# Sums of weight quarters put on VectorE one operand ahead of use, and the high parts of computed down operands put later in ScalarE's queue

## The chip, the cores and the metric

One core of a Trainium2 chip runs the whole program. The metric is the device time of one execution in microseconds (us); lower is better.

## What is computed

A two-layer encoder runs over 768 tokens (a prompt of 256 and a sample of 512, which share all weights) with width 1024. In each layer a gated convolution branch and an attention branch are mixed and added to the stream, and a feed-forward part (FFN) of width 2816 follows. The change bears on the FFN only:

```
for l in range(DEPTH):
    ...
    x = x + (ga * a + gc * c) @ w_out[l]
    h2 = rms_norm(x, g_ffn[l])
    gate, up = jnp.split(h2 @ w_gu[l], 2, axis=-1)
    x = x + (jax.nn.silu(gate) * up) @ w_down[l]
return rms_norm(x, g_final)
```

All of it is in float32.

## The kernel before

**Split products.** A float32 matrix product is made of three matmuls on parts that TensorE takes in one pass: each operand is split into a high part (ScalarE copies it into the reduced type, `act` at L211) and a low part (the operand minus its high part, `sub_lo` at L214, on GpSimd for weights and on VectorE for most activations). VectorE's calls go through the wrapper class `Vector`, so all of them have line L133.

**Seven products.** In the FFN, a product of 2x2 blocks is computed with seven block products in place of eight (m = 1 to 7). Four of the seven weight operands (m = 4, 5, 6, 7) are sums or differences of quarters of two staged weight tiles. `Quad.total` (L273) makes such a sum on VectorE, 128x512, in a tile T of pool tag H (6 slots), once per quad. `Quarter.make` (L259) asks for its operand (L260), so that a missing sum goes into VectorE's queue at that point, and then puts the high part on ScalarE (L263) and the low part on GpSimd (L264).

**Order of work.** The program is one stream of blocks, and the Python code keeps a planner's clock (`Clock`): each matmul adds its planned length, and after each step of a block (six matmuls of 384 columns, planned 0.96 us, or twelve) `tick` runs the jobs that are due and then `Weights.pump` (L337), which loads weight tiles and prepares at most one weight quarter per tick (`split`, L325) if there is room: eight quarters may be ready ahead of use. All engines run their queues in order, so what the planner puts first runs first.

**The FFN's blocks.** `gu_body` (L1025) computes one 128-wide chunk of gate and up per block: the tiles are named f0 to f21 by chunk (the first two chunks share a block, f0), with twelve matmuls for each of the seven products, in the order m = 1, 7, 6, 4, 5, 2, 3. Products 6, 5 and 3 are added into the PSUM bank of product 1, and product 4 into that of product 7. So the matmuls of m=6 wait until ScalarE has copied product 1 out (`L_silu`), those of m=4 until it has copied product 7 out (`L_fu`, L1053), those of m=5 until it has copied the bank after m=6 (L1055), and those of m=3 until VectorE has added the bank after m=5 into `L_fu` (L1060).

**Down products.** After every four chunks the down product of these four is computed in four bursts (a to d) between the following chunks: burst a (m = 1, 7) stands before f4, f8, f12, f16 and f20, burst b (6, 4) behind that chunk, then c (5, 2) and d (3). `down7` (L1115) prepares their moving operands. `prepare(m)` (L1136) makes, for m = 7, 6, 5 and 3, two differences or sums on VectorE (tiles `L_dS`, `L_silu`), and `high` (L1142) puts two high parts `L_dh` on ScalarE, from which two low parts `L_dl` on VectorE follow. For these four products `high` is due D_HIGH planner microseconds after `prepare`; for m = 1, 2, 4, whose operands exist already, it is due at once:

```
jobs[m].append(clock.later(0.0 if m in (1, 2, 4) else D_HIGH, high))
```

The results of down products are added into the residual tiles `L_x` by VectorE, four or eight additions of 128x384 per product.

**Start of the FFN.** The operands of the seven products (tiles `L_h`, from `L_hs` and `L_hr`) are made on VectorE, ScalarE and GpSimd by `ffn_norm` (L920) while the block f0 is being computed.

Names of tiles in the profile: `wq_L_wgu_0m` and `wq_L_wd4b_0m` are the high and low parts of quarters of the gate/up weights and of the weights of burst b of the chunks 4 to 7; `T_L_wgu` and `T_L_wd4b` are the sums; `st_...` are the staged weight tiles.

Of the kernel before, what the change touches and what calls it, by code (L numbers as in the profile page):

```python
# [44 lines left out]
CONV_N = ZP - 2 * PAD  # L45
# [8 lines left out]
class Clock:  # L54
# [21 lines left out]
    def tick(self):  # L76
        while self.heap and self.heap[0][0] <= self.now:
            heapq.heappop(self.heap)[2]()
        while self.dve < self.now + TAP_AHEAD and self.tap():
            pass  # L80
# [38 lines left out]
class Vector:  # L119
# [5 lines left out]
    def __getattr__(self, name):  # L125
        f = getattr(self.engine, name)

        def call(out, *args, **kw):
            n = 1
            for d in (args[0].shape if name == "tensor_reduce" else out.shape)[1:]:  # L130
                n *= d
            self.clock.vector(n / 960.0 + 0.13)
            return f(out, *args, **kw)  # L133
        return call

# [20 lines left out]
def trunk(tc, x_in, x_tok, w_a, w_qkv, w_pw, w_out, w_gu, w_down, vecs, gqk, rope, y_out):  # L156
# [4 lines left out]
    with ExitStack() as ctx:  # L161
# [51 lines left out]
        def sub_lo(engine, lo, x, hi):  # L213
            engine.tensor_tensor(lo, x, hi.bitcast(F32), op=ALU.subtract)  # L214
# [73 lines left out]
        class Weights:  # L288
# [36 lines left out]
            def split(self, engines=(nc.gpsimd,)):  # L325
                w = self.all[self.ready]
                while not self.here(w):
                    assert self.load()
                assert self.live + w.size + max(self.staged, N_WS) <= N_W
                self.live += w.size  # L330
                w.live = True
                w.make(engines)
                self.staged -= sum(stage.last is w for stage in w.stages)
                self.ready += 1
                self.next = max(self.next, clock.now + W_STEP[w.size - 1])

            def pump(self):  # L337
                while self.load():
                    pass
                if self.ready < len(self.all) and clock.now >= self.next:  # L340
                    w = self.all[self.ready]
                    if self.here(w) and self.live + w.size + max(self.staged, N_WS) <= N_W:
                        self.split()
# [285 lines left out]
        def layer_blocks(l):  # L629
# [485 lines left out]
            def down7(c0):  # L1115
# [20 lines left out]
                def prepare(m):  # L1136
# [5 lines left out]
                    def high():  # L1142
                        ops[m] = U(nm(f"dh{c0}_{m}"), F32R), U(nm(f"dl{c0}_{m}"), F32R)
                        for e, x in enumerate(src[m]):
                            hi, lo = (half(t, e) for t in ops[m])
                            act(hi, x)
                            jobs[m].append(clock.later(D_LOW + 0.5 * e, lambda x=x, hi=hi, lo=lo: sub_lo(vector, lo, x, hi)))
                    jobs[m].append(clock.later(0.0 if m in (1, 2, 4) else D_HIGH, high))

# [464 lines left out]
D_AT = 0.5  # L1614
D_EACH = 2.5
D_TAIL = 2.0
D_HIGH = 0.7
D_LOW = 0.8
A_SPLIT = (15.0, 1.5)

# [17 lines left out]
RSTD_AFTER = 5.4  # L1638
TABLES_AT = 16.0
TAP_AHEAD = 1.0  # L1640
W_STEP = (0.9, 2.9)
A_EXP = 2.2
A_REC = (4.5, 2.5)
# [91 lines left out]
```

## Time and profile before

| | |
|---|---|
| median of 3 runs | 2401.75 us (2399.19 to 2402.68) |
| the profiled execution's own time | 2401.79 us |
| its span, first to last instruction | 2400.0 us |
| TensorE busy | 2235.7 us, 93% |
| VectorE busy | 1933.2 us, 81% |
| GpSimd busy | 1285.0 us, 54% |
| ScalarE busy | 1134.3 us, 47% |
| mean granted TensorE clock | 0.972 of full speed |

The FFN of the first layer takes about 670 to 1190 us of the span, that of the second about 1858 to 2380 us. Busy time is that of instructions on the engine; "idle before" is time in which the engine had nothing running, with the instruction that ended it.

### The profile page before, as it was taken

Reading aid. Unit: us, or ns where it says so; the run is one execution under the profiler, and the core shown is the slowest. Engines: PE = TensorE matmul, PEld = TensorE weight load, DVE = VectorE, ACT = ScalarE, POOL = GpSimd, SP = SyncE. Lnnn points to the kernel's source line nnn. Section 1 sums busy time; section 2 is a strip of 40 time slices with the busy share of each in tenths; the row PEclk is TensorE's granted clock in tenths of the full one; section 3 lists DMA queues with packets and bytes.
Section 4 is the critical chain, followed back from the end, with each engine's and each line's share of the span. In section 5 each row is a group of like instructions: output and inputs, shape, how many; then the busy total and the mean of one; then the engine's idle time right before and its main releaser. Section 6 shows DMA issues by size and latency. Waiting matters only on the chain. (4 is left out here: it accounts for less than half of the span.)

```text
span 2400.0 us, 34938 instructions
## 1 busy us (share of the span) xinstructions
PE 2235.7 (93%) x13276; PEld 2101.9 (88%) x13276; DVE 1933.2 (81%) x2480; ACT 1134.3 (47%) x2281; POOL 1285.0 (54%) x956
## 2 busy tenths in 40 slices
PE   8888898999979999999998899999999799999997
PEld 7878787888979999999987788878889799999997
DVE  5899999855387798798978999997553887887888
ACT  5425564684244444444443255647843444444443
POOL 4933554442266666666668344535323766756664
PEclk9999999999989999999999899999999899999999
DMA  4111111133313343343421111112341133334332
GB/s 168 36 62 62 52 58 60 64 101 137 113 44 110 119 141 123 124 141 110 156 82 53 53 47 57 58 62 78 111 170 53 44 121 135 129 118 141 123 123 88
DMA packets 72425, 229.60 MB, mean 96 GB/s; under 512 B 8128, under 2 KB 15296, under 8 KB 72256
## 3 DMA queue, kind: packets, MB, share of 16 engines
q1 hardware_dynamic: 72256, 227.37, 27.7%
q8 instruction: 104, 1.70, 0.3%
q14 instruction: 65, 0.53, 0.1%
HBM read 208.46 MB, written 18.87 MB: 95 GB/s over the span
## 5 line engine op out<-in xcount | busy, mean ns | idle before, releaser
L133 DVE SCALAR_TENSOR_TENSOR L_y<-L_z,vec,L_y 128x783 f32<-128x783 f32 x480 | 638.7, 1363 | 2.5
L214 POOL TENSOR_TENSOR wq_L_wgu_0m<-T_L_wgu,wq_L_wgu_0m 128x512 fp32r<-128x512 f32 x168 | 228.5, 1375 | 172.5 <-ACT wq_L_wgu_0m L211 172.5
L211 ACT ACTIVATE wq_L_wgu_0m<-T_L_wgu 128x512 fp32r<-128x512 f32 x168 | 102.7, 630 | 257.6 <-DVE T_L_wgu L133 204.4
L214 POOL TENSOR_TENSOR wq_L_wgu_0m<-st_L_wgu,wq_L_wgu_0m 128x512 fp32r<-128x512 f32 x126 | 179.3, 1424 | 43.3 <-ACT wq_L_wgu_0m L211 42.6
L203 PE MATMUL L_gl<-L_h1h,hi_L_wgl 128*128 128x512 f32 (+1 forms) x512 | 181.5, 355 | 0.3 <-DVE L_q3r L133 0.2
L203 PE MATMUL L_gl<-L_h1h,lo_L_wgl 128*128 128x512 f32 (+1 forms) x512 | 176.1, 344 | 0.0
L203 PE MATMUL L_gl<-L_h1l,hi_L_wgl 128*128 128x512 f32 (+1 forms) x512 | 176.0, 344 | 0.0
L214 POOL TENSOR_TENSOR lo_L_wgl<-st_L_wgl,hi_L_wgl 128x1024 fp32r<-128x1024 f32 x32 | 87.8, 2745 | 147.1 <-ACT hi_L_wgl L211 116.5
L214 POOL TENSOR_TENSOR lo_L_wqkv<-st_L_wqkv,hi_L_wqkv 128x1024 fp32r<-128x1024 f32 x24 | 69.0, 2877 | 137.1 <-ACT hi_L_wqkv L211 132.1
L214 POOL TENSOR_TENSOR lo_L_wu<-st_L_wu,hi_L_wu 128x1024 fp32r<-128x1024 f32 (+1 forms) x32 | 85.9, 2685 | 61.4 <-ACT hi_L_wu L211 61.4
L203 PEld LDWEIGHTS L_gl<-L_h1h,lo_L_wgl 128*128 128x128 f32 x512 | 99.0, 193 | 11.6
L203 PEld LDWEIGHTS L_gl<-L_h1h,hi_L_wgl 128*128 128x128 f32 x512 | 99.3, 194 | 10.7 <-DVE L_q3r L133 0.7
L203 PEld LDWEIGHTS L_gl<-L_h1l,hi_L_wgl 128*128 128x128 f32 x512 | 99.2, 194 | 10.3 <-issue 0.5
L214 POOL TENSOR_TENSOR lo_L_wo<-st_L_wo,hi_L_wo 128x1024 fp32r<-128x1024 f32 x16 | 39.6, 2476 | 116.0 <-ACT hi_L_wo L211 116.0
L203 PE MATMUL L_ua<-L_h1h,lo_L_wu 128*128 128x256 f32 (+1 forms) x256 | 89.0, 348 | 6.2 <-POOL lo_L_wu L214 6.1
L133 DVE TENSOR_TENSOR L_dl<-L_silu,L_dh 128x384 fp32r<-128x384 f32 x80 | 59.5, 782 | 41.0 <-ACT L_dh L211 41.0
L214 POOL TENSOR_TENSOR lo_L_wpw<-st_L_wpw,hi_L_wpw 128x1024 fp32r<-128x1024 f32 x16 | 40.0, 2502 | 97.0 <-ACT hi_L_wpw L211 92.2
L203 PE MATMUL L_ug<-L_h1h,lo_L_wu 128*128 128x256 f32 (+1 forms) x256 | 88.6, 346 | 2.3 <-DVE lo_L_wu L133 2.3
L203 PE MATMUL L_c<-L_zsh,hi_L_wpw 128*128 128x256 f32 (+1 forms) x256 | 90.4, 353 | 0.0
L203 PE MATMUL L_ug<-L_h1h,hi_L_wu 128*128 128x256 f32 (+1 forms) x256 | 89.8, 351 | 0.0
L203 PE MATMUL L_ua<-L_h1h,hi_L_wu 128*128 128x256 f32 (+1 forms) x256 | 89.8, 351 | 0.0
L211 ACT ACTIVATE wq_L_wgu_0m<-st_L_wgu 128x512 fp32r<-128x512 f32 x126 | 78.6, 623 | 22.9 <-POOL wq_L_wgu_0m L214 19.1
(1630 smaller groups left out, 7882.9 us busy)
## 6 DMA issues: line engine op xcount, KB each, us to landing
st_L_wgu<-w_gu SPq DMA_DIRECT2D x88, 512.0 KB, 3.5
st_L_wu<-w_a SPq DMA_DIRECT2D x32, 512.0 KB, 3.8
st_L_wgl<-w_a SPq DMA_DIRECT2D x32, 512.0 KB, 3.5
st_L_wqkv<-w_qkv SPq DMA_DIRECT2D x24, 512.0 KB, 3.6
st_L_wpw<-w_pw SPq DMA_DIRECT2D x16, 512.0 KB, 3.7
st_L_wo<-w_out SPq DMA_DIRECT2D x16, 512.0 KB, 3.7
g_dram<-L_sgl SPq DMA_DIRECT2D x16, 384.0 KB, 2.5
L_gj<-g_dram SPq DMA_DIRECT2D x16, 384.0 KB, 4.1
```

Source lines behind the costliest of these rows:

```text
L133: return f(out, *args, **kw)
L203: nc.tensor.matmul(out, lhsT, rhs, start=start, stop=stop)
L211: nc.scalar.activation(out, in_, func, **kw)
L214: engine.tensor_tensor(lo, x, hi.bitcast(F32), op=ALU.subtract)
```

## The change

`split` now ends by asking for the operand of the next quarter in line, if that unit is a quarter (size 1) and its stages have been loaded. Where this operand is a sum, the sum is put on VectorE there, one `split` earlier than before; where the next quarter needs none, or has it, nothing is issued. D_HIGH goes from 0.7 to 2.4. The constant TAP_MORE in the planner's price of a 783-wide VectorE call equals the 0.13 that stood there.

```diff
-            self.clock.vector(n / 960.0 + 0.13)
+            self.clock.vector(n / 960.0 + (TAP_MORE if n == CONV_N else 0.13))
...
                 self.ready += 1
                 self.next = max(self.next, clock.now + W_STEP[w.size - 1])
+                if self.ready < len(self.all):
+                    then = self.all[self.ready]
+                    if then.size == 1 and self.here(then):
+                        then.quad.operand(then.m)
...
-D_HIGH = 0.7
+D_HIGH = 2.4
...
 TAP_AHEAD = 1.0
+TAP_MORE = 0.13
```

## Rows read from the trace of the kernel before

**Rows 1.** The page: busy time by engine, and one of its costliest groups.

```profile
PE 2235.7 (93%) x13276; PEld 2101.9 (88%) x13276; DVE 1933.2 (81%) x2480; ACT 1134.3 (47%) x2281; POOL 1285.0 (54%) x956
...
L211 ACT ACTIVATE wq_L_wgu_0m<-T_L_wgu 128x512 fp32r<-128x512 f32 x168 | 102.7, 630 | 257.6 <-DVE T_L_wgu L133 204.4
```

**Rows 2.** Busy time by stretch (stretch, its length, engines, clock, DMA share, GB/s).

```profile
674.00:724.00 50.00, 35.50 (x157) 33.01 (x158) 44.67 (x53) 21.16 (x42) 34.56 (x27) 0.83 0.13 42
846.00:869.50 23.50, 21.39 (x121) 20.64 (x120) 23.09 (x32) 9.24 (x18) 13.59 (x11) 1.00 0.36 126
...
860.00:951.00 91.00, 88.76 (x504) 87.81 (x504) 75.33 (x102) 40.77 (x79) 58.76 (x43) 1.00 0.37 127
```

Engines stand in the order PE, PEld, DVE, ACT, POOL.

**Rows 3.** Waits of TensorE (us in total over the run, times, longest).

```profile
PE L_f00m L475 <- POOL L_h L214: 20.7, 9, 2.8
...
PE L_f40m L475 <- ACT L_fu L211: 2.9, 2, 1.6
PE L_f160m L475 <- ACT L_fu L211: 2.8, 2, 1.4
...
PE L_f80m L475 <- ACT L_fu L211: 2.0, 2, 1.4
...
PE L_f40m L475 <- ACT L_silu L211: 1.5, 2, 0.8
...
PE L_f130m L475 <- ACT L_silu L211: 0.3, 1, 0.3
```

**Rows 4.** Timeline of TensorE around chunk 8 (start, length, instruction, idle before).

```profile
860.85 2.34 PE L475 MATMUL L_f80m<-L_h,wq_L_wgu_0m 128*128 128x384 f32 x12 [1.36 <-ACT L_fu L211]
863.95 6.53 PE L475 MATMUL L_f80m<-L_h,wq_L_wgu_0m 128*128 128x384 f32 x36 [0.76 <-ACT L_silu L211]
870.32 0.34 PE L1181 MATMUL L_d4m<-L_dh,wq_L_wd4b_0m 128*128 128x384 f32 x1
```

**Rows 5.** Timeline of ScalarE in the same stretch.

```profile
857.81 0.53 ACT L211 ACTIVATE L_dh<-L_dS 128x384 fp32r<-128x384 f32 x1 [1.68 <-DVE L_dS L133]
...
860.33 0.47 ACT L211 ACTIVATE L_fu<-L_f80m 128x384 f32<-128x384 f32 x1
...
862.89 0.63 ACT L211 ACTIVATE wq_L_wd4b_0m<-T_L_wd4b 128x512 fp32r<-128x512 f32 x1 [1.27 <-DVE T_L_wd4b L133]
863.43 0.47 ACT L211 ACTIVATE L_silu<-L_f80m 128x384 f32<-128x384 f32 x1
```

**Rows 6.** Timeline of VectorE in the same stretch.

```profile
845.61 0.56 DVE L133 TENSOR_TENSOR L_silu<-L_f70m,L_silu 128x384 f32<-128x384 f32 x1 [0.76 <-PE L_d4m L1181]
846.08 1.73 DVE L133 TENSOR_TENSOR T_L_wgu<-st_L_wgu 128x512 f32<-128x512 f32 x1
...
852.13 1.83 DVE L133 TENSOR_TENSOR T_L_wgu<-st_L_wgu,T_L_wgu 128x512 f32<-128x512 f32 x1
...
856.68 2.67 DVE L133 TENSOR_TENSOR L_dS<-L_silu,L_dS 128x384 f32<-128x384 f32 x2
859.27 1.22 DVE L133 TENSOR_TENSOR L_dl<-L_dS,L_dh 128x384 fp32r<-128x384 f32 x2
...
866.61 0.68 DVE L133 TENSOR_TENSOR T_L_wd4b<-st_L_wd4b,T_L_wd4b 128x512 f32<-128x512 f32 x1
867.21 0.55 DVE L133 TENSOR_TENSOR L_fu<-L_f80m,L_fu 128x384 f32<-128x384 f32 x1
867.67 1.33 DVE L133 TENSOR_TENSOR T_L_wd4b<-st_L_wd4b,T_L_wd4b 128x512 f32<-128x512 f32 x1
```

**Rows 7.** Timeline of GpSimd: a low part of weights beside VectorE's sum at 852.13.

```profile
852.11 1.31 POOL L214 TENSOR_TENSOR wq_L_wgu_0m<-T_L_wgu,wq_L_wgu_0m 128x512 fp32r<-128x512 f32 x1 [2.17 <-ACT wq_L_wgu_0m L211]
```

**Rows 8.** Timeline of VectorE at the start of the first FFN.

```profile
678.38 1.30 DVE L133 TENSOR_TENSOR T_L_wgu<-st_L_wgu,st_L_wgu 128x512 f32<-128x512 f32 x1
680.57 1.48 DVE L133 TENSOR_TENSOR L_hs<-L_hs,L_n2R 128x384 f32<-128x384 f32 x3 [0.89 <-PE L_n2R L207]
...
719.97 1.39 DVE L133 TENSOR_TENSOR T_L_wgu<-st_L_wgu,T_L_wgu 128x512 f32<-128x512 f32 x1
```

## The prediction

> **What bounds the kernel now.** I read the page first. TensorE is busy for 93% of the span, and ScalarE loses 204.4 us in front of high parts of summed quarters because VectorE's sum is not there yet [rows 1]. That is the wait which the change takes away. But ScalarE is busy for only 47%, so its idle time is worth nothing in itself; what counts is where TensorE waits for ScalarE, and the waits of TensorE say where [rows 3]. In the FFN there are two kinds. In the chunks f4, f8, f12, f16 and f20 of each layer, those behind a burst a, the matmuls of m=4 wait for the copy `L_fu` and those of m=5 for the copy `L_silu`. The chunk f12 has a row for `L_fu` like that of f8, and f20 one like that of f16, so `L_fu` costs 2.9 + 2 x 2.0 + 2 x 2.8 = 12.5 us over both layers, and `L_silu` 5 x 1.5 = 7.5 us. Together they are 20.0 us at ten places. At the start of each FFN TensorE waits for the low parts `L_h`, 20.7 us in nine waits, and there its mean granted clock is 0.83, so part of the time it runs at 1.2 GHz [rows 2, 3]. Around chunk 8 and over the group of four chunks behind it the clock is 1.00, the 2.4 GHz level [rows 2], so the ten places cost their idle time and nothing more.
>
> Then I read the timelines of one place, chunk 8, in the order TensorE, ScalarE, VectorE. TensorE stands for 1.36 us in front of m=4 and for 0.76 us in front of m=5 [rows 4], 2.12 us in all. ScalarE's queue says why: the copy at 860.33 stands behind two `L_dh` that waited for `L_dS` (the first for 1.68 us, to 857.81), and the copy at 863.43 behind a high part that waited 1.27 us for its sum [rows 5]. The part to keep in mind is VectorE: over the chunk's 23.5 us it is busy for 23.09 us, while over the whole group of four chunks, 91 us, it is busy for 75.33 us [rows 2]. At this very place, then, VectorE has no time to give.
>
> **The change, part by part.** TAP_MORE equals the constant it replaces: nothing moves in the convolution stage, and no instruction is added or removed anywhere. SyncE's queue keeps its order of loads, and a staged tile that a sum reads comes free earlier, never later. A sum holds its slot of tag H one `split` longer; the idle times ahead of sums name no wait for a slot [rows 6, 8], so I cost this at nothing. Sums move up by one `split`, `L_dh` (with the `L_dl` behind it) moves down.
>
> *D_HIGH.* `prepare(6)` falls into the first tick of a chunk behind burst a. With 0.7 the two `L_dh` go into ScalarE's queue at the end of m=1; with 2.4 they go there at the end of m=7, behind the copy `L_fu`. That copy then needs only TensorE and can run as soon as m=7 ends, two microseconds ahead of its need. The 1.36 us go. What is queued behind the late high parts: their low parts, which move behind the sums of burst b's first quarters. Burst b starts at 870.32 [rows 4], and the first two of these low parts now end at 860.49 [rows 6], so delays of up to 9.8 us are covered. The same holds for the operands of m=7, 5 and 3; the chunks in front of bursts a, c and d show at most 0.3 us of such waits [rows 3].
>
> *Sums one ahead.* ScalarE's high part at 862.89 would find its sum made. So the copy at 863.43 is no longer held by it, and the 0.76 us in front of m=5 can go too. Upper end of the saving per place: 2.12 us.
>
> *What is late next.* The matmuls of m=3 wait for VectorE's addition of m=5, which ends at 867.76 [rows 6]. The 36 matmuls of m=5, 2 and 3 take 870.32 - 863.95 = 6.37 us [rows 4], 2.12 us per product, so m=3 starts at 868.20 now: a slack of 0.44 us. If TensorE comes 2.12 us earlier, this addition must come 1.68 us earlier, from an engine without idle time. So I count what its queue holds ahead of the addition. One sum leaves: that at 846.08 (1.73 us) goes up in front of the idle 0.76 us at 845.61. One sum enters: that at 867.67 (0.68 to 1.33 us) now stands ahead of the addition [rows 6]. All others change places among themselves. A sum takes 0.68 us alone and 1.83 us where it meets a low part on GpSimd, as at 852.13 [rows 6, 7]. Best case: the leaving sum fits wholly into the idle time and the entering one runs alone, 1.73 - 0.68 = 1.05 us earlier. Worst without more meetings: 0.97 us of the leaving sum stay behind the idle time and the entering one takes 1.33, so 1.73 - 0.97 - 1.33 = 0.57 us later. TensorE's saving at one place is the slack plus this: between -0.13 and 1.49 us. I take the middle, 0.68 us, as rows 6 show short and long sums about equally often, and over ten places 6.8 us, with -1 and 15 us as ends.
>
> *Small waits.* The chunk behind each of the ten has a wait of at most 0.3 us of the second kind [rows 3]; I take 1 us of at most 3 us over all, and nothing is the other end.
>
> *Start of the FFN.* Here the first sum of m=5 (678.38, 1.30 us) goes up into time in which VectorE waits, and the second takes its place; 0.89 us of idle time still follow [rows 8]. Behind that the number of sums ahead of each `L_h` stays the same, so ScalarE stops waiting for sums while VectorE's queue keeps its pace. At the end a fourth sum of the next chunk comes ahead of the last `L_h`, behind the one at 719.97 [rows 8], which costs 0.68 to 1.83 us. For the gain the nearest row is the idle 0.89 us and the 1.30 us sum, 2.2 us at most per layer. I take 1 us per layer, and from -1.8 to +2.2 us as ends: 2 us in all, ends -3.7 and 4.4.
>
> *Sum.* 6.8 + 1 + 2 = 9.8 us. The profiled execution took 2401.79 us (its span is 2400.0) and the median of the runs is 2401.75 us, so the sum can be set against either: 2392 us. With all terms at their ends it is 2379 to 2407 us.
>
> **The rule that speaks against it.** The low part on GpSimd ran from 852.11 for 1.31 us and the sum from 852.13 for 1.83 us, so the sum ended 0.54 us after the low part, less than the 0.68 us that it takes alone [rows 6, 7]. They stood in each other's way, but not for the whole length. The Trainium skill (SBUF — State Buffer, section "SBUF: two separate sides") says that VectorE instructions with two SBUF inputs and GpSimd instructions exclude each other for a whole instruction. By that rule the chunk would have no room for any gain, which is rival B below; by the rows a little is left.
>
> **Rivals.** *A, both waits go in full.* It needs the addition of m=5 to come 1.68 us earlier at each place, so more than the 1.05 us counted: one meeting with GpSimd fewer (1.15 us, the difference of 1.83 and 0.68) would do. For it speaks that sums and low parts no longer follow each other in lockstep through ScalarE's wait; against it that GpSimd's work then falls elsewhere on the same 23 us. Price: 20.0 + 3 + 4.4 = 27.4 us, 2374 us.
>
> *B, the place is full.* Count the stretch from 846.0 to 869.5: eleven low parts on GpSimd at 1.31 us are 14.4 us; the ten sums on VectorE (first 846.08, last 867.67) are 6.8 us alone, and two `L_dS`, four `L_dl` and one product with two SBUF inputs are some 4.3 us at the 0.61 us of the row at 859.27 [rows 2, 6, 7]. That is 25.5 us in 23.5 us, so what is not hidden side by side already fills it, and the wait for ScalarE turns into one for VectorE of the same size. Only the start of the FFN gains: 2400 us, no measurable change. The page named above is the rule for this case; the trace agrees in direction, not in size.
>
> *C, slower: sums stand ahead of the addition that TensorE needs.* If the moved sums meet GpSimd once more per place than now, the addition comes 0.57 + 1.15 = 1.72 us later, and m=3 starts 1.72 - 0.44 = 1.28 us later than now, ten times; with the start's 3.7 us that is 16.5 us, 2418 us. It decides from 0.44 us of lateness on. Against it: the count of meetings in this stretch is high already.
>
> *D, the change does little as written.* If the next quarter's stages were not loaded at `split`, the sum would stay where it is, and only D_HIGH would act: the 12.5 us of `L_fu` are then the limit, with the same limit by VectorE. This falls into B or the forecast.
>
> **Numbers.** The measurement of this kernel can tell 0.2%, 4.8 us. Forecast (4.8 to 18 us gained): 0.52. A: 0.17. B, with D: 0.19. C: 0.12. Faster is the forecast and A, 0.69; the same 0.19; slower 0.12. The range reaches from A, 2374 us, past no change to 2404 us, 0.1% above it, and leaves C out. The forecast's own range is 2382 to 2398 us.
>
> **What would show it.** In the profile after: ScalarE's wait for sums falls from 204.4 us to a small rest; `L_fu` of chunk 8 stands ahead of the `L_dh` and m=4 starts without a wait. The forecast asks for a new wait of TensorE in f4, f8 and so on, for `L_fu` from VectorE (the addition), of about 1.4 us in place of 2.12. No such wait would be A; one of over 2.1 us would be B or C. Wrong altogether would be a change in the stretches outside the FFN, or a first wait for `T_L_wgu` or a staged tile on TensorE's path.

## The result, and the profile after

The changed kernel is slower: 2414.81 us (median of 4 runs, 2410.20 to 2417.68) against 2401.89 us for the kernel before (4 runs, 2399.19 to 2402.68), a ratio of 1.0054 with a 95% interval of 1.0041 to 1.0066. The forecast was 2392 us, and its range ended at 2404.

The page of the profiled execution (2413.32 us, span 2411.5) answers to [rows 1]:

```profile
PE 2246.1 (93%) x13276; PEld 2114.4 (88%) x13276; DVE 1943.3 (81%) x2480; ACT 1140.7 (47%) x2281; POOL 1312.2 (54%) x956
...
L211 ACT ACTIVATE wq_L_wgu_0m<-T_L_wgu 128x512 fp32r<-128x512 f32 x168 | 104.9, 630 | 243.2 <-DVE T_L_wgu L133 97.4
```

ScalarE's wait for these sums fell from 204.4 to 97.4 us, so the change does what it says, but only by half and not to the small rest that was forecast; and all idle time in front of these high parts fell only from 257.6 to 243.2 us, since they now wait longer for TensorE's bursts (26.8 us for `L_d4m` alone, 16.0 before). The time did not follow. TensorE is busy for 10.4 us more with the same 13276 matmuls, the first sign that some of them run slower. TensorE's waits, as in [rows 3]:

```profile
PE L_f00m L479 <- POOL L_h L214: 17.6, 9, 4.1
...
PE L_f00m L479 <- DVE L_h L133: 4.8, 4, 1.8
...
PE L_f80m L479 <- DVE L_fu L133: 3.6, 2, 1.8
...
PE L_f40m L479 <- DVE L_x L133: 0.7, 2, 0.4
```

The waits for `L_fu` and `L_silu` from ScalarE at the ten places are gone without rest. In their place each of the five chunks f4, f8, f12, f16 and f20 has the same row as f8, a wait of 1.8 us per layer for `L_fu` from VectorE, and one of 0.2 to 0.4 us for `L_x`, for which the kernel before has none, ahead of the chunk. TensorE's timeline at chunk 8, first the start of the chunk in the kernel before, then the changed kernel in the first and in the second layer (columns as in [rows 4]):

```profile
852.97 6.53 PE L475 MATMUL L_f80m<-L_h,wq_L_wgu_0m 128*128 128x384 f32 x36
```

```profile
857.37 12.80 PE L479 MATMUL L_f80m<-L_h,wq_L_wgu_0m 128*128 128x384 f32 x72 [0.23 <-DVE L_x L133]
871.95 2.36 PE L479 MATMUL L_f80m<-L_h,wq_L_wgu_0m 128*128 128x384 f32 x12 [1.78 <-DVE L_fu L133]
874.14 0.34 PE L1185 MATMUL L_d4m<-L_dh,wq_L_wd4b_0m 128*128 128x384 f32 x1
...
2062.52 3.59 PE L479 MATMUL L_f80m<-L_h,wq_L_wgu_0m 128*128 128x384 f32 x12 [1.81 <-DVE L_fu L133]
2065.91 0.53 PE L1185 MATMUL L_d4m<-L_dh,wq_L_wd4b_0m 128*128 128x384 f32 x1
```

Both places of the changed kernel wait equally long, but the same 12 matmuls of m=3 take 874.14 - 871.95 = 2.19 us in the first layer and 2065.91 - 2062.52 = 3.39 us in the second. The windows say why (columns as in [rows 2]; the first is the start of the FFN, the second chunk 8, the third its group, the last two follow the wait at 2062.52):

```profile
676.60:726.60 50.00, 34.88 (x153) 31.25 (x154) 45.96 (x54) 22.36 (x45) 38.11 (x29) 0.82 0.13 42
850.40:873.90 23.50, 21.50 (x122) 20.89 (x121) 23.11 (x34) 10.77 (x21) 14.05 (x10) 1.00 0.29 102
864.40:955.40 91.00, 88.97 (x509) 88.36 (x508) 76.88 (x101) 41.10 (x77) 60.62 (x42) 1.00 0.39 129
...
2063.40:2066.60 3.20, 3.20 (x12) 3.20 (x11) 2.25 (x4) 0.98 (x2) 3.00 (x2) 0.50 0.80 251
2066.60:2078.00 11.40, 11.40 (x67) 11.40 (x66) 10.40 (x14) 3.10 (x6) 7.15 (x5) 1.00 0.07 26
```

Behind the wait the granted clock is 0.50, the 1.2 GHz level, over a stretch of 3.2 us, and then 1.00 again. This happens at five of the ten places of this execution (f20 in the first layer, f8, f12, f16 and f20 in the second) and at none in the execution of before.

Why does TensorE wait for the addition? It is not late beside the kernel before: it ends 871.89 - 857.37 = 14.52 us after the first matmul of the chunk, and 867.76 - 852.97 = 14.79 us before the change. But TensorE now comes to it 2.6 us earlier, after 12.80 us (before, at 868.20, m=3 followed m=2 without a wait, and the last matmul of m=2 ends 0.17 us into it: 15.40 us). So the question is what keeps the addition where it is. ScalarE's timeline and then VectorE's in chunk 8, to be read beside [rows 5] and [rows 6]:

```profile
861.84 0.49 ACT L211 ACTIVATE L_fu<-L_f80m 128x384 f32<-128x384 f32 x1 [0.27 <-PE L_f80m L479]
862.23 0.93 ACT L211 ACTIVATE L_dh<-L_dS 128x384 fp32r<-128x384 f32 x2
...
864.90 0.47 ACT L211 ACTIVATE L_silu<-L_f80m 128x384 f32<-128x384 f32 x1
...
870.39 0.63 ACT L211 ACTIVATE wq_L_wd4b_0m<-T_L_wd4b 128x512 fp32r<-128x512 f32 x1 [4.07 <-DVE T_L_wd4b L133]
```

```profile
861.71 1.78 DVE L133 TENSOR_TENSOR T_L_wd4b<-st_L_wd4b 128x512 f32<-128x512 f32 x1
...
864.97 0.69 DVE L133 TENSOR_TENSOR T_L_wd4b<-st_L_wd4b,T_L_wd4b 128x512 f32<-128x512 f32 x1
865.58 1.66 DVE L133 TENSOR_TENSOR L_dl<-L_dS,L_dh 128x384 fp32r<-128x384 f32 x1
867.16 1.66 DVE L133 TENSOR_TENSOR L_dl<-L_silu,L_dh 128x384 fp32r<-128x384 f32 x1
868.74 0.55 DVE L133 TENSOR_TENSOR L_dl<-L_dS,L_dh 128x384 fp32r<-128x384 f32 x1
869.21 0.55 DVE L133 TENSOR_TENSOR L_dl<-L_silu,L_dh 128x384 fp32r<-128x384 f32 x1
869.67 0.68 DVE L133 TENSOR_TENSOR T_L_wd4b<-st_L_wd4b,T_L_wd4b 128x512 f32<-128x512 f32 x1
...
871.34 0.55 DVE L133 TENSOR_TENSOR L_fu<-L_f80m,L_fu 128x384 f32<-128x384 f32 x1
```

`L_fu` now stands ahead of the `L_dh`, as foretold. But the four `L_dl` that belong to them, which burst b needs only later, take VectorE from 865.58 to 869.76, and behind them stand the addition (871.34) and the sum for which ScalarE waits 4.07 us. In the kernel before, the four took 2.2 us ([rows 6], and 1.01 us for two from 862.72). Two of them run for 1.66 us instead of 0.55, beside two low parts on GpSimd:

```profile
865.08 1.74 POOL L214 TENSOR_TENSOR wq_L_wd4b_0m<-T_L_wd4b,wq_L_wd4b_0m 128x512 fp32r<-128x512 f32 x1 [2.13 <-ACT wq_L_wd4b_0m L211]
866.78 1.61 POOL L214 TENSOR_TENSOR wq_L_wd4b_1m<-T_L_wd4b,wq_L_wd4b_1m 128x512 fp32r<-128x512 f32 x1
```

The start of the FFN, first TensorE, then VectorE, whose last sum here in the kernel before is in [rows 8]:

```profile
721.35 0.95 PE L479 MATMUL L_f00m<-L_h,wq_L_wgu_0m 128*128 128x384 f32 x3 [1.81 <-POOL L_h L214]
723.94 1.01 PE L479 MATMUL L_f00m<-L_h,wq_L_wgu_0m 128*128 128x384 f32 x2 [1.64 <-DVE L_h L133]
724.75 4.04 PE L479 MATMUL L_f01m<-L_h,wq_L_wgu_1m 128*128 128x384 f32 x12
```

```profile
721.64 1.78 DVE L133 TENSOR_TENSOR T_L_wgu<-st_L_wgu,T_L_wgu 128x512 f32<-128x512 f32 x1
723.34 0.55 DVE L133 TENSOR_TENSOR L_h<-L_hr,L_h 128x384 fp32r<-128x384 f32 x1
```

A fourth sum, at 721.64, stands ahead of the last `L_h`, TensorE waits 1.64 us for it, and the 12 matmuls behind, at a granted clock of 0.50, take 4.04 us instead of 2.23.

To see where the time went I cut each trace at the first matmuls of chunks and of norms. "Start" is f0 to f4 in both layers, "chunks" f4 to the next norm in both layers, "rest" all else, where every engine has the same instructions in the same order in all kernels. In us:

| kernel | start | chunks | places with 1.2 GHz | rest | median of runs |
|---|---|---|---|---|---|
| before | 183.7 | 858.1 | 0 | 1358.2 | 2401.9 |
| after | 189.3 | 861.1 | 5 | 1361.1 | 2414.8 |
| e1_high_only | 184.9 | 863.3 | 0 | 1357.4 | 2407.8 |
| e2_sums_only | 189.4 | 855.6 | 0 | 1355.6 | 2404.0 |
| e3_lows_late | 187.8 | 850.4 | 0 | 1360.0 | 2399.5 |
| e4_filler | 190.2 | 853.3 | 0 | 1356.6 | 2402.3 |
| e5_start_off | 186.2 | 867.6 | 9 | 1360.9 | 2410.9 |
| e6_start_lows | 184.9 | 850.8 | 0 | 1356.8 | 2395.1 |
| e7_start_order | 184.9 | 848.8 | 0 | 1357.9 | 2395.3 |
| e8_before_order | 184.0 | 865.8 | 0 | 1356.1 | 2408.4 |
| e9_pool_lows | 186.1 | 846.8 | 0 | 1357.6 | 2392.3 |
| e10_before_filler | 183.6 | 864.1 | 0 | 1358.0 | 2409.2 |
| e11_behind_b | 184.8 | 847.1 | 0 | 1358.4 | 2393.1 |

The rest differs by up to 5.5 us between executions although nothing in it was edited, so a single profile is compared by its own stretches, and kernels by their medians. In the eleven profiles other than those of the changed kernel and of e5_start_off, no place of the 110 runs at 1.2 GHz. The two spans differ by 11.5 us: 5.6 in the start, 3.0 in the chunks, 2.9 in the rest.

### The profile page after: what moved, and what is told of

It is laid out like the page before. It is cut to its first block, busy times and chain, and to the rows that moved or that the text cites. A ratio compares the mean times of both kernels' runs of the same rounds, so it can differ in the third digit from the quotient of the medians.

```text
span 2411.5 us, 34937 instructions
## 1 busy us (share of the span) xinstructions
PE 2246.1 (93%) x13276; PEld 2114.4 (88%) x13276; DVE 1943.3 (81%) x2480; ACT 1140.7 (47%) x2281; POOL 1312.2 (54%) x956
## 5 line engine op out<-in xcount | busy, mean ns | idle before, releaser
L214 POOL TENSOR_TENSOR wq_L_wgu_0m<-T_L_wgu,wq_L_wgu_0m 128x512 fp32r<-128x512 f32 x168 | 236.7, 1412 | 156.0 <-ACT wq_L_wgu_0m L211 155.0
L211 ACT ACTIVATE wq_L_wgu_0m<-T_L_wgu 128x512 fp32r<-128x512 f32 x168 | 104.9, 630 | 243.2 <-DVE T_L_wgu L133 97.4
L214 POOL TENSOR_TENSOR wq_L_wgu_0m<-st_L_wgu,wq_L_wgu_0m 128x512 fp32r<-128x512 f32 x126 | 187.7, 1490 | 45.7 <-ACT wq_L_wgu_0m L211 45.6
L133 DVE TENSOR_TENSOR T_L_wgu<-st_L_wgu,T_L_wgu 128x512 f32<-128x512 f32 x88 | 118.9, 1351 | 4.0
L133 DVE TENSOR_TENSOR L_dl<-L_silu,L_dh 128x384 fp32r<-128x384 f32 x80 | 73.8, 953 | 37.2 <-ACT L_dh L211 36.4
```

Of the source, the lines that this page charges most:

```text
L211: nc.scalar.activation(out, in_, func, **kw)
```

## The experiments

**e1_high_only: the late high parts alone.**

```diff
-D_HIGH = 0.7
+D_HIGH = 2.4
```

> The kernel before with D_HIGH at 2.4 alone; sums stay where they were. My theory (VectorE's queue ahead of the addition for m=5 decides in the chunks behind a burst a): the waits for L_fu and most of that for L_silu from ScalarE go, the wait before m=3 for the addition L_fu becomes about 1.2 us in place of 1.8, since one sum fewer stands ahead of it; the start of the FFN is as before, and as the waits are split up, TensorE's clock stays at 2.4 GHz there. Time about 2397 us, 4 us under the kernel before. Rival (the late high parts do the harm, by their low parts): slower than before by 5 us or more, with a wait before m=3 of 1.8 us or more.

Measured: 2407.76 us, ratio 1.0026 (1.0017 to 1.0036): slower, and the expectation missed. The rival's time came, but not its wait: in front of m=3 TensorE waits 0.4 us, not 1.8. TensorE's waits at f8:

```profile
PE L_f80m L475 <- DVE L_fu L133: 0.8, 2, 0.4
PE L_f80m L475 <- ACT L_fu L211: 0.8, 2, 0.6
...
PE L_f80m L475 <- ACT L_silu L211: 0.7, 2, 0.4
...
PE L_f80m L475 <- DVE L_x L133: 0.3, 1, 0.3
```

Two waits of a place have become three or four, of 0.2 to 0.6 us. In the chunks TensorE's idle times over 0.1 us went from 22.4 us in 30 waits to 19.6 us in 56, yet the chunks take 5.2 us more. A wait costs more than the idle time of its row: matmuls start 0.174 us apart but last 0.34 us, so 0.17 us of drain comes ahead of the idle time, and the 12 matmuls behind the wait at 871.95 take 2.19 us instead of 12 x 0.174 = 2.09. With these 0.27 us per wait, an estimate from the rows, 26 more waits are 7.0 us, less 2.8 of idle time 4.2 us, most of the 5.2 measured; the chunks themselves would give (5.2 + 2.8) / 26 = 0.31 us.

**e2_sums_only: the sums ahead alone.** The changed kernel with

```diff
-D_HIGH = 2.4
+D_HIGH = 0.7
```

> The changed kernel with D_HIGH back at 0.7; only the sums move. My theory: the start of the FFN keeps its loss (3 to 5 us over both layers), and in the chunks behind a burst a TensorE waits both for L_fu from ScalarE (m=4, about 1 us) and for VectorE's addition (m=3, about 1 us); the two waits are short, so the clock stays up there. Time 2402 to 2408 us, above the kernel before. Rival (the sums are the good part and the high parts the bad one): 2390 us or less.

Measured: 2403.99 us, ratio 1.0009 (1.0000 to 1.0018), inside the expected range. The place showed another picture than expected: no wait for ScalarE at m=4, but again one for VectorE's addition, of 1.3 to 1.4 us at eight of the ten places and of 1.8 us at the two of f4:

```profile
PE L_f80m L479 <- DVE L_fu L133: 2.6, 2, 1.4
...
PE L_f70m L479 <- DVE L_fu L133: 2.1, 2, 1.1
```

So sums ahead alone free ScalarE and turn the wait over to VectorE; with D_HIGH it is 1.8 us at all ten places. The second row is a wait that the changed kernel does not have: f7, f11, f15 and f19, ahead of a burst a, wait 1.0 to 1.1 us for the addition in both layers, some 8 us in all. So the late high parts have a good half as well, and a bad one: the waits for `L_x` ahead of f8, f12, f16 and f20 are absent here, and e1 has them. The start keeps its full loss (189.4 us), which puts that loss on the sums.

**e3_lows_late: the low parts of burst b's operands later.** The changed kernel with

```diff
-jobs[m].append(clock.later(D_LOW + 0.5 * e, lambda x=x, hi=hi, lo=lo: sub_lo(vector, lo, x, hi)))
+jobs[m].append(clock.later((D_LOW_B if m in (6, 4) else D_LOW) + 0.5 * e, lambda x=x, hi=hi, lo=lo: sub_lo(vector, lo, x, hi)))
...
+D_LOW_B = 5.5
```

> The changed kernel, with the four low parts L_dl of burst b put behind the addition for m=5 in VectorE's queue (5.5 planner us after their high parts in place of 0.8). My theory (that queue decides): the 1.8 us wait before m=3 goes at all ten places, and with it the stretch at 1.2 GHz behind it; at most 0.5 us comes back as a wait of burst b for a low part. Time about 2392 us, 20 us or more under the changed kernel. Rival (the place is full whatever the order): the wait moves to burst b, 1.5 us or more at each place, and the time stays within 5 us of the changed kernel.

Measured: 2399.53 us, ratio 0.9990 (0.9981 to 0.9999), 15 us under the changed kernel by one delay. The wait before m=3 is gone and no place runs at 1.2 GHz, so the four `L_dl` were what held the addition back. The second half of the expectation, that burst b would wait 0.5 us at most, missed, and with it the 2392 us:

```profile
869.34 0.34 PE L1185 MATMUL L_d4m<-L_dh,wq_L_wd4b_0m 128*128 128x384 f32 x1
...
871.57 0.45 PE L1185 MATMUL L_d4m<-L_dl,wq_L_wd4b_1m 128*128 128x384 f32 x1 [1.37 <-DVE L_dl L133]
```

**e4_filler: six matmuls done twice at each place.** The changed kernel, in `seven`; what is computed is the same, since the first product of m=2 starts its bank anew afterwards:

```diff
+                if m == 2 and name in FILLED:
+                    for k in range(2):
+                        for p, (a, b) in enumerate(PASSES):
+                            nc.tensor.matmul(ps, w[a][:, k * P:(k + 1) * P], h.cols(m, k, b), start=True, stop=True)
```

> The changed kernel, in which TensorE does the first six matmuls of m=2 twice in the ten chunks behind a burst a (1.04 us of work each, ahead of the 1.8 us wait); the second time starts the bank anew, so the results are the same. My theory of the clock (one wait of 1.8 us lets the clock fall to 1.2 GHz for the matmuls behind it, in about half of the ten places, 1.6 us each; two shorter waits did not): the wait shrinks to 0.8 us, the addition still ends at the same time, no clock stretch follows, and the kernel is 5 to 9 us faster than the changed one, for 60 matmuls more. Rival (the clock at these places is chance and not the wait): no gain, the same time as the changed kernel within 3 us and clock stretches as before.

Measured: 2402.26 us, 12.5 us under the changed kernel with 60 matmuls more, where 5 to 9 us were expected. The wait is cut short, not the work:

```profile
PE L_f80m L483 <- DVE L_fu L133: 1.5, 2, 0.8
```

At 0.8 us no place runs at 1.2 GHz. Six matmuls (6 x 0.174 = 1.04 us) cost as much as the wait lost (1.78 - 0.8), so the two kernels differ at a place by the clock alone: f8 to f12 of the second layer takes 92.13 us after and 90.59 us here, f12 to f16 92.02 and 90.44. That is 1.56 us per place, 7.8 us for five. In the first layer, where the changed kernel kept its clock, the two take the same: 90.61 and 90.61 us from f8 to f12, 90.56 and 90.58 from f12 to f16. The two profiled spans differ by 11.4 us, 7.8 in the chunks and 4.5 in the rest, where nothing was edited, less 0.9 in the start. So 7.8 of the 12.5 us are shown to be the clock's at these places. Of what is left, part can be executions in which more than five places fell; the runs do not say how many in each.

**e5_start_off: no sums ahead for the first two blocks of an FFN.** The changed kernel with

```diff
-if then.size == 1 and self.here(then):
+if then.size == 1 and self.here(then) and not any(s in then.name for s in START):
...
+START = ("wgu0", "wgu2_")
```

> The changed kernel, but for the weights of the first two blocks of each FFN (f0 with f1, and f2) no sum is put ahead. Theory (the FFN start loses because sums now stand in front of the low parts L_h on VectorE and GpSimd): the stretch from f0 to f2 falls from 55.8 and 56.4 us to about 54.2, that from f2 to f4 from 38.3 and 38.8 to about 37.6, 5.6 us in all, so 2409 us; the wait of 1.8 us before m=3 at the ten places stays, with half-speed stretches behind some of them. Rival (the loss comes from the clock or from the late high parts, not from these sums): the two stretches keep their length and the time is 2413 to 2416 us.

Measured: 2410.87 us (6 runs, 2402.25 to 2416.39), ratio 1.0039 (1.0024 to 1.0055), which its interval does not part from the changed kernel's. In the profile the start gave back 3.2 of the 5.6 us expected (54.0 and 55.3 us from f0 to f2); f2 to f4 nearly stayed (38.3 and 38.5). In the profiled execution, the longest of the six, nine of the ten places run at 1.2 GHz, with the same waits of 1.8 us as after. Nine times 1.56 us are 14.0 us, and the six runs span 14.1 us; e6_start_lows, with no such place, spans 2.5 us in nine runs. The mean granted clock of the six runs goes down as their time goes up, in order, from 0.971 at 2402.25 us to 0.965 at 2416.39 us, while in e6 it stays between 0.971 and 0.974. So how many places fall seems to change from execution to execution; that is read from one profile, the spread and these means, and not counted in each run.

**e6_start_lows: e3_lows_late and e5_start_off together.**

> The kernel of e3_lows_late, again with no sum ahead for the first two blocks of each FFN. Theory: without half-speed stretches the start's loss shows alone, 1.4 + 0.7 us in the first layer and 1.5 + 0.6 us in the second, 4.1 us, so 2395.4 us against 2399.5. Rival (the start's loss is not from these sums): 2399 to 2400 us.

Measured: 2395.06 us, ratio 0.9974 (0.9965 to 0.9984), 4.5 us under e3_lows_late: the size was hit, the split only in part. From f0 to f2 it takes 54.15 and 54.20 us, as before, so sums ahead were that loss (2.9 us). From f2 to f4 it stays 0.65 us longer than before. That is no part of the FFN's start: it is the new wait for `L_x` (0.4 us, and its drain) that closes this stretch in front of f4.

**e7_start_order: the low parts of m=6 directly behind the addition, those of m=4 behind the products.** The kernel of e6_start_lows with

```diff
-jobs[m].append(clock.later((D_LOW_B if m in (6, 4) else D_LOW) + 0.5 * e, lambda x=x, hi=hi, lo=lo: sub_lo(vector, lo, x, hi)))
+jobs[m].append(clock.later(D_LOW_B.get(m, D_LOW + 0.5 * e), lambda x=x, hi=hi, lo=lo: sub_lo(vector, lo, x, hi)))
...
-D_LOW_B = 5.5
+D_LOW_B = {6: 5.5, 4: 6.8}
```

> As e6_start_lows, but the two low parts of m=6 stand directly behind the addition of m=5 in VectorE's queue, and those of m=4 behind the two products L_silu. Theory (in e3_lows_late burst b waited 1.4 us only because the second low part of m=6 stood behind L_silu<-L_fu, 1.63 us): that wait falls to 0.4 us or less, so 10 us less over the ten places, 2385 us; TensorE shows no wait over 0.5 us between the start of chunk 4 and the norm. Rival (VectorE is full there, and what is moved is only late elsewhere): the wait goes to the low parts of m=4 inside burst b or to the next chunk's L_silu, and the time is 2394 to 2396 us.

Measured: 2395.30 us, ratio 0.9978 (0.9970 to 0.9987), no better than e6_start_lows. Burst b no longer waits, but the next chunk does:

```profile
PE L_f90m L479 <- DVE L_x L133: 2.4, 2, 1.2
```

The rival was right: VectorE is behind, and a low part moved out of TensorE's way delays an addition `L_x`, whose bank chunk f9 needs.

**e8_before_order: the same late high and low parts, without any sum ahead.** The kernel before with D_HIGH = 2.4 and the low parts of e7_start_order.

> The kernel before with late high parts (2.4) and the order of low parts of e7_start_order, but no sum ahead anywhere. Theory (each half of the change takes one of ScalarE's two waits, and the low parts in front of the addition took the gain back): VectorE's two waits of e1_high_only (0.39 and 0.36 us) go, ScalarE's two (0.55 and 0.38 us) stay, so about 1.1 us per place with restarts against 2.3 before, 2390 us, some 5 us over e7_start_order. Rival (sums ahead do nothing for TensorE once the low parts are out of the way): the time of e7_start_order within 2 us, with no wait for ScalarE at m=4 and m=5.

Measured: 2408.41 us, ratio 1.0032 (1.0020 to 1.0044): both expectations missed, by 18 and 13 us. TensorE at chunk 8:

```profile
854.54 4.46 PE L475 MATMUL L_f80m<-L_h,wq_L_wgu_0m 128*128 128x384 f32 x24 [0.36 <-DVE L_x L133]
859.50 2.35 PE L475 MATMUL L_f80m<-L_h,wq_L_wgu_0m 128*128 128x384 f32 x12 [0.50 <-ACT L_fu L211]
862.22 6.54 PE L475 MATMUL L_f80m<-L_h,wq_L_wgu_0m 128*128 128x384 f32 x36 [0.37 <-ACT L_silu L211]
```

The same small waits come in the chunks around it: 57 waits with 21.9 us in the chunks, against 30 with 22.4 before. By the price of e1, 27 x 0.27 - 0.5 = 6.8 us of the 7.7 us that the chunks lose. Against e7_start_order the sums ahead are worth 13 us. They are the good half of the change once the low parts are out of the way.

**e9_pool_lows: the low parts of m=4 on GpSimd.** As e7_start_order, with f3 left out of the sums ahead too:

```diff
-D_LOW_B = {6: 5.5, 4: 6.8}
+D_LOW_B = {6: 5.5, 4: 5.5}
...
-sub_lo(vector, lo, x, hi)
+sub_lo(nc.gpsimd if m == 4 else vector, lo, x, hi)
...
-START = ("wgu0", "wgu2_")
+START = ("wgu0", "wgu2_", "wgu3_")
```

> As e7_start_order, but the two low parts of m=4 are computed on GpSimd, ahead of the last low part of burst b's weights, and the chunk f3 has no sums ahead either. Theory (VectorE is the full engine at the ten places, GpSimd has room): VectorE loses two low parts of 0.55 us between the addition and the additions L_x, so the wait of 1.2 us that e7_start_order has behind burst b falls to 0.4 us or less, 8 us over the ten places, and the start gains 1.2 us more: 2386 us. Rival (GpSimd's two more instructions slow VectorE's by as much, or make burst b's weights late): a wait of a microsecond stays per place, on VectorE or as one for GpSimd, and the time is 2392 to 2397 us.

Measured: 2392.30 us, ratio 0.9960 (0.9947 to 0.9974). The wait in front of f9 went from 1.2 to 1.0 us, not to 0.4:

```profile
PE L_f90m L479 <- DVE L_x L133: 2.0, 2, 1.0
```

VectorE lost 1.0 us of work, but two of its sums behind the addition now run for 1.3 us beside GpSimd instead of 0.68. The rival's mechanism held, though its median lies 3 us under that of e7_start_order. Leaving out f3 did nothing (f2 to f4: 38.27 us). It is the fastest kernel of the study, 0.4% under before.

**e10_before_filler: the same 60 matmuls in the kernel before.**

> The kernel before with the same 60 filler matmuls as e4_filler. Theory (in e4_filler they made the changed kernel faster because they cut the single wait of 1.8 us short and so kept the clock at 2.4 GHz): here no half-speed stretch lies at the ten places and no wait stands behind them, so they cost their own time, 60 x 0.174 = 10.4 us, 2412 us, and at least 2408. Rival (the fillers help by something else, such as time for VectorE): 2402 us or less.

Measured: 2409.15 us, ratio 1.0031 (1.0020 to 1.0043), 7.2 us slower, above the least that was expected (2408), though not the full 10.4 us: in the chunks they cost 6.1 us. The ten chunks take 0.98 us longer each, nearly the whole of the six matmuls, but the chunk behind each takes 0.37 us less: its waits for `L_silu` of up to 0.3 us [rows 3] are gone. The other waits for ScalarE stay about as in [rows 3]. So repeated matmuls cost time where the clock is up and gain it where they keep it up.

**e11_behind_b: no sums ahead in the chunks behind a burst b either.** As e9_pool_lows, with those five chunks added to START.

> As e9_pool_lows, but the chunks behind a burst b (f5, f9, f13, f17, f21) have no sums ahead either: one sum less stands ahead of the fifth addition L_x, for which TensorE waits 1.0 us at each of the ten places. Theory (those sums are what is ahead of the additions): the wait falls to 0.3 us or less, 7 to 9 us less in all, 2384 us. Rival (without sums ahead ScalarE waits again, and with it TensorE inside f5, f9 and so on, as in e8_before_order): 0.6 us or more for L_fu or L_silu in those chunks, 2390 to 2396 us.

Measured: 2393.10 us, ratio 0.9961 (0.9948 to 0.9975), the same as e9_pool_lows. The wait for `L_x` went, and ScalarE's came back, as the rival said:

```profile
PE L_f90m L479 <- ACT L_fu L211: 1.0, 2, 0.5
...
PE L_f90m L479 <- ACT L_silu L211: 0.4, 2, 0.2
```

## Why the prediction was wrong

It was right on who would wait for whom: ScalarE's waits at the ten places vanish, and TensorE waits in front of m=3 for VectorE's addition instead. Four steps failed. By the forecast the span would have been 2400.0 - 9.8 = 2390.2 us; the profiled one, 2411.5, lies 21.3 us above it: 7.8 us of the clock, 3.0 that the chunks gained less, 7.6 of the start, and 2.9 in the rest, which no edit touched.

**"So the ten places cost their idle time and nothing more."** For the kernel before it was a right reading; the step that failed was to price the new wait in the same way. Without that the two kernels would have been about level (4.8 us gained in the chunks, 5.6 lost in the start). The clock of 1.00 was read around chunk 8 of the kernel before, where 2.12 us of idle time come in two pieces, 1.36 and 0.76 us, with 12 matmuls between. The change puts nearly as much into one piece of 1.8 us, and behind that the clock falls at some places: 1.56 us each, 7.8 us in the profiled execution. e4 and e10 show it: the same matmuls gain 12.5 us in one kernel and cost 7.2 in the other. That the length of the one piece counts and not the sum of the two is argued, not shown; no run has the same idle time in one piece and in two. I should have asked what shape the new wait has. The Trainium skill (TensorE: Matmul & The Clock Gate, section "HAM oscillation — how this bites in real kernels") tells of a kernel in which waits between bursts of matmuls put TensorE back to the low clock each time. The waits there are for DMA, and longer than these; the trace shows the same, with 0.50, behind waits of 1.8 us, at five places of ten.

**The saving per place, 0.68 us (6.8 us, and 1 us of small waits).** Without the clock the chunks gain 858.1 - (861.1 - 7.8) = 4.8 us instead of 7.8. Where the clock stayed up, a chunk behind a burst a takes 16.80 us instead of 17.21 from its first matmul to burst b, so 0.41 us are saved per place; the chunk behind it takes 0.46 us less, not the 0.1 of the small waits. Against that stands a term that the sum does not have, the new wait for `L_x`: 0.2 to 0.3 us and 0.17 of drain, 3.3 us for the eight that lie in the chunks; the two in front of f4 (1.3 us) still have to be paid in the start.

The wait for the addition is 1.78 us, not 1.44, and not because the addition came later than forecast. At chunk 8 it comes 0.27 us earlier than before, and the forecast's middle was 0.24. TensorE comes 2.6 us earlier, not 2.12, since the two waits that went had cost more than their idle time. That the addition came as forecast is luck: I counted the sums in VectorE's queue and let the rest "change places among themselves", and what changed was who meets GpSimd. From burst a to the addition ten sums take 9.1 us, where nine took 10.6, and the four `L_dl` take 4.4 us, not the 0.61 us each that rival B prices. I had covered their delay by burst b's need, which is right, and left out that they stand ahead of the addition. e3 shows the cost of that: with them behind it, the chunks take 10.7 us less, the clock's part among them. The Trainium skill's rule on VectorE and GpSimd (SBUF — State Buffer, section "SBUF: two separate sides"), that one waits for the whole instruction of the other, is nearly what these rows show too: the `L_dl` of 865.58 ends 0.42 us after GpSimd's low part, 0.13 less than the 0.55 it takes alone; in the row that I weighed the rule with, 0.14 were missing (0.54 of 0.68).

**The start, 1 us gained per layer.** It lost 5.6 us in all, of which 1.3 belong to the wait in front of f4. The loss that I named, a fourth sum ahead of the last `L_h`, came at 721.64 (1.78 us) near the top of its bounds, and it cost more than itself, since 12 matmuls behind the wait ran at 1.2 GHz: 4.04 us instead of 2.23 before. e6 takes the sums away and has 54.2 us from f0 to f2, as before. The gain set against it does not show.

**A wait costs its idle time.** The sum counted 2.12 us less 1.44. A wait costs some 0.27 us beyond its row (e1, e8), so the change should have gained from having fewer waits; this error lies on the other side and is small here, but it made TensorE's new wait longer than forecast, and it made me miss e1 and e8.

Of the rivals, C had the right sign and nearly the right time (2418), but by luck: it has the addition 1.72 us later, by sums that meet GpSimd, and no clock. At chunk 8 the addition came 0.27 us earlier, it was the low parts that met GpSimd more than before, and the clock made the larger part of the loss. B was right that VectorE's place is full: e7, e9 and e11 move work around it, and each time another wait of about a microsecond appears. A is not reached by any kernel here; the fastest, e9_pool_lows, comes to 2392.3 us, the forecast's time, but only with three further edits. Two slips in the working change nothing: B's eleven low parts take in one that ends at 846.01, so ten are 13.1 us and B's sum 24.2 us, still over the 23.5; and a gain of 4.8 to 18 us is 2384 to 2397 us, not 2382 to 2398.

What stays open: why the clock falls behind some waits of 1.8 us and not behind others of the same length, how many places fall in each execution of the changed kernel, and the 2.9 us of the rest.

## What to carry to other kernels

When a wait is moved to another engine, ask for the shape of the new wait as well as its sum: here two waits that left the clock at 2.4 GHz became one that at half of its places did not, and the matmuls behind it paid. Work that is put ahead in a full queue should be followed by a look at what in that queue is not yet needed; here delaying four low parts was worth 15 us, the clock's part among them, more than the whole change was meant to gain. A spread of times that goes with the granted clock, as in the six runs of e5 (14.1 us, 0.971 down to 0.965), is a sign that the clock falls in some runs and not in others. The spread alone is none: the four runs after spread by 7.5 us, but so do 32 runs of the kernel before (7.4 us).

## What the runs showed of the hardware that was not expected

- A single wait of 1.8 us between matmuls was followed by 3.2 us at 1.2 GHz at five of ten places, and at nine in an execution of a kernel with the same waits (e5); waits of 1.36 and 0.76 us with 12 matmuls between, one of 1.4 us (e2, e3), one of 0.8 us (e4) and the two of 1.8 us in e2 were not. The Trainium skill (TensorE: Matmul & The Clock Gate, section "What's actually happening") says that the number of slow matmuls at the start of one kernel varies between its runs; the 14.1 us spread of e5 fits that, for places far behind the start.
- 60 matmuls more made a kernel 12.5 us faster (e4; 7.8 us of it are shown to be the clock's), and the kernel before 7.2 us slower (e10).
- Waits cost some 0.3 us each beyond their idle time, an estimate from the rows of e1 and e8: 56 waits with 19.6 us cost more than 30 with 22.4 us (e1).
- GpSimd's low parts of weights run for 1.3 us alone, and also where they begin just ahead of a two-input instruction of VectorE (852.11 in [rows 7]); where such an instruction was already running they took 1.74 and 1.61 us (865.08 and 866.78 here). VectorE's `L_dl` go from 0.55 to 1.66 us beside them.
